# A hybrid encoder on one core: the sample's conv layer norm on the untransposed block, with its statistics sent through DRAM

## The chip, the core and the metric

The kernel runs on one core of one Trainium2 chip. A core has a matmul engine (PE, TensorE) and, beside it, DVE (VectorE), ACT (ScalarE) and POOL (GpSimd); SP (SyncE) issues nearly all DMAs of this kernel. Each engine takes its own instructions in order and waits on semaphores for the others. Matmul results land in PSUM, which is cut into eight banks of 128 x 512 numbers here; everything else is in SBUF, with 128 partitions. The metric is the time of one execution on the device, in microseconds.

## What is computed

One layer of an encoder, for two requests with the same weights: the prompt (512 tokens) and the sample (1024 tokens), in float32. The part that the change touches is the convolution branch.

```
def _layernorm(x, g, b):                     # over the 512 channels of one token
    mu = mean(x); xc = x - mu
    return xc * rsqrt(mean(xc * xc) + EPS) * g + b

h = rmsnorm(x); z = h @ w_in                 # q, k, v, ca, cb
a_out = window_attention(q, k, v)            # 512 channels
c = ca * sigmoid(cb)
c = dwconv(c, conv_dw_w, conv_dw_b)          # 31 taps along the tokens
c = silu(_layernorm(c, conv_ln_g, conv_ln_b))
x = x + concat([a_out, c]) @ w_out           # 1024 channels
h = rmsnorm(x); u = dwconv3(h @ w_up)        # 2 x 2816 channels
x = x + (silu(u_gate) * u_value) @ w_down
y = rmsnorm(x)
```

## The kernel before

Every float32 matmul is made of three: operands are split into a rounded high half and the rest (`hi`, `lo`), and hi x hi, hi x lo and lo x hi are summed in PSUM. ACT casts the high half, DVE or POOL subtracts for the low one.

The prompt's tokens are blocks 0 to 3 of 128 tokens, the sample's are blocks 4 to 11. First the input projection runs for all, then attention and the output projection of the prompt, then the prompt's up-projection (`up_half`, L983 and L987 its three-tap convolution) beside which the sample's attention (`scores`, `values`: L655 scores, L697 transposes, L711 and L712 values, L719 to L723 the result into `cat`) and the sample's long convolution run. Then come the sample's output projection (`out_half`, L813 to L815 on PE, one block and one half of the 1024 columns at a time, L819 adds the residual), and a long second half: up-projection and down-projection of the sample, both in a form with fewer products (L1249 to L1251 and L1612 to L1614 on PE).

The long convolution runs with channels on partitions; the sample's result goes to DRAM (`cvd`) in four chunks of 128 channels. The layer norm needs statistics over channels. `conv_norm(i)` therefore does the following for a block of 128 tokens:

- it loads the block from `cvd` into `held`, four chunks of (128 channels x 128 tokens), and the attention half from `catd`;
- L760: four transposes on PE turn it to tokens on partitions, into a PSUM bank `pt`;
- L765, L766: mean and variance per token on DVE; `rstd_of` (L147, L148) makes the reciprocal root on POOL;
- L769: DVE subtracts the mean and multiplies by the root, one number per partition each, into `xh`;
- after YN = 2 yields (other work is recorded between), L775: four transposes turn `xh` back to channels on partitions, into a second bank `p2`;
- L781: ACT applies gain and bias per channel, for the sample also putting the tokens in order (even and odd tokens were kept apart by the convolution); L782 to L785 make the swish and the two halves `cat[0]` (hi, by ACT's cast L784) and `cat[1]` (lo, L785 on DVE). The output projection reads these as its stationary operand for channels 512 to 1023 (kc 4 to 7).

The generator `fitted(i)` runs `conv_norm` for a sample block; blocks 4 and 5 are normalised in `tail()`, beside the end of the up-projection, blocks 6 to 11 in the loop over `turns_out`, NE = 2 blocks ahead of their output projection. The transposes use the bank `c` for blocks 4 and 5, then the banks `a`. Up to the second half a scheduler, which lists instructions by a model of their times, sets the order of each engine's instructions, PE's and SP's among them; only from the sample's up-projection on is PE's order fixed by hand. Tiles take slots of four sizes (`q`, `c`, `h`, `d`, and `s` for small ones), and a slot is free again when its holder is dropped.

Of the kernel before, what the change touches and what calls it, by code (L numbers as in the profile page):

```python
# [9 lines left out]
F32 = mybir.dt.float32  # L10
# [3 lines left out]
ALU = mybir.AluOpType  # L14

P = 128
# [8 lines left out]
CCH = 512  # L25
# [30 lines left out]
YN = 2  # L56
# [53 lines left out]
def tile_hybrid_encoder(ctx: ExitStack, tc: tile.TileContext, xs, rel_bias, norm_attn_g, w_in,  # L110
                        attn_sink, conv_dw_w, conv_dw_b, conv_ln_g, conv_ln_b, w_out, norm_ffn_g,
                        w_up, ffn_dw_w, ffn_dw_b, w_down, norm_final_g, onehot, laid, outs):
    nc = tc.nc
# [3 lines left out]
    dr = ctx.enter_context(tc.tile_pool(name="dr", bufs=1, space=bass.MemoryType.DRAM))  # L117
# [4 lines left out]
    sb = Slots(lambda tag: sml if tag[0] == "s" else big,  # L122
               dict(q=(15, 4096), c=(4, 4352), h=(61, 2048), d=(2, 2304), s=(33, 64)))
# [3 lines left out]
    def sm(n):  # L127
        return sb.tile([n])

    def bank(job):  # L130
        return banks.tile([NT], among=use[job])
# [8 lines left out]
    ident = cst.tile([P, P], F32, name="ident")  # L140
# [5 lines left out]
    def rstd_of(ss, n, out):  # L146
        nc.gpsimd.tensor_scalar(out, ss, 1.0 / n, EPS, op0=ALU.mult, op1=ALU.add)  # L147
        nc.gpsimd.tensor_tensor(out, out, nhalf[:, :out.shape[1]], op=ALU.pow)  # L148
# [95 lines left out]
    for _ in range(NW // 4):  # L244
        pt = bank("step")
        for i in range(4):
            nc.tensor.transpose(pt[:, i * P:(i + 1) * P], ident[:], ident[:])
        pt = None
# [60 lines left out]
    def drain(queue):  # L309
        while queue:  # L310
            advance(mid[0] if mid else queue)
# [368 lines left out]
    def cat_of(i, part):  # L680
        if (i, part) not in cats:
            cats[i, part] = (sb.tile([4, P], F32R), sb.tile([4, P], F32R))
        return cats[i, part]
# [55 lines left out]
    def load_cat(i):  # L739
        cats[i, 0] = (sb.tile([4, P], F32R), sb.tile([4, P], F32R))  # L740
        for L in range(2):
            nc.sync.dma_start(cats[i, 0][L][:].bitcast(F32), catd[blocks[i][1], :, L, :].rearrange("p (j t) -> p j t", t=P))

    def conv_norm(i):
        G, b = blocks[i]
        if G["g"] == 0:
            drain(convs)
        cat = cat_of(i, 1)
        if G["g"] == 0:
            cv = [kept[c][:, b * P:(b + 1) * P] for c in range(4)]  # L750
        else:
            held = sb.tile([4, P])
            nc.sync.dma_start(held[:].rearrange("p c (h k) -> p c h k", h=2), cvd[:, b])
            cv = [held[:, c, :] for c in range(4)]
            if (i, 0) not in cats:
                load_cat(i)
            yield 0.0
        pt = bank("norm")
        for c in range(4):
            nc.tensor.transpose(pt[:, c * P:(c + 1) * P], cv[c], ident[:])  # L760
        if G["g"] == 0 and b == G["nb"] - 1:
            kept.clear()
        held = None
        st, mv, rs = sm(6), sm(2), sm(1)
        nc.vector.bn_stats(st[:], pt[:])  # L765
        nc.vector.bn_aggr(mv[:], st[:])  # L766
        rstd_of(mv[:, 1:2], 1.0, rs[:])
        xh = sb.tile([CCH])
        nc.vector.tensor_scalar(xh[:], pt[:], mv[:, 0:1], rs[:], op0=ALU.subtract, op1=ALU.mult)  # L769
        del pt  # L770
        for _ in range(YN):
            yield 0.0
        p2 = bank("norm")
        for c in range(4):
            nc.tensor.transpose(p2[:, c * P:(c + 1) * P], xh[:, c * P:(c + 1) * P], ident[:])  # L775
        y, t = sb.tile([4, P]), sb.tile([4, P])
        for c in range(4):
            o, n = y[:, c, :], p2[:, c * P:(c + 1) * P]
            if G["g"] == 1:
                o, n = o.rearrange("p (k h) -> p h k", h=2), n.rearrange("p (h k) -> p h k", h=2)  # L780
            nc.scalar.activation(o, n, AF.Identity, scale=lng[:, c:c + 1], bias=lnb[:, c:c + 1])  # L781
        nc.scalar.activation(t[:], y[:], AF.Tanh)  # L782
        nc.vector.scalar_tensor_tensor(t[:], t[:], 1.0, y[:], op0=ALU.add, op1=ALU.mult)
        nc.scalar.copy(cat[0][:], t[:])  # L784
        nc.vector.tensor_tensor(cat[1][:], t[:], cat[0][:].bitcast(F32), op=ALU.subtract)  # L785
        yield 0.0
# [99 lines left out]
    def normed(i):  # L886
        yield from conv_norm(i)
        ready.add(i)
# [155 lines left out]
    def fitted(i):  # L1044
        yield from conv_norm(i)
        fit.add(i)
# [258 lines left out]
    st = {}  # L1305
# [610 lines left out]
```

## Time and profile before

| What | Value |
|---|---|
| median of 3 runs | 1481.91 us (1481.87 to 1482.33) |
| profiled execution, its own time | 1484.05 us |
| profiled execution, its span | 1482.1 us |
| mean granted clock of PE | 0.998 |
| DMA traffic | 228.17 MB, mean 154 GB/s |
| DMA, mean share of 16 engines, 630 to 650 us | 0.77 to 1.05 by stretches of 5 us |

Times in the profile are microseconds from the span's start. A timeline row has start, length, engine, line, operation, output and inputs by slot class, and in brackets how long the engine stood idle before it and what ended that. The chain row of a piece gives what it added to the chain of work that ended last. A row of the windows' table gives busy time and count of PE, of its weight loads, of DVE, ACT and POOL, then the granted clock as a share of full speed, the DMA share and GB/s.

### The profile page before, as it was taken

What the parts mean: (1) busy time and instruction counts of PE and PEld (TensorE: products, weight loads), DVE (VectorE), ACT (ScalarE), POOL (GpSimd) and SP (SyncE); (2) the same over time, 40 slices, a digit from 0 to 9 for tenths busy, and PEclk for the clock granted to TensorE, in tenths of its full rate; (3) what the DMA queues carried; (4) which work ended last, traced back from release to release, by engine and by line L of the source; (5) the groups of instructions that cost most, each with busy time, mean ns of one, the idle gap of its engine ahead of it and who ended that gap; (6) DMA issues with size and microseconds to landing.
All of it is one profiled execution on the core that took longest, in us unless ns stands there. A gap on an engine that the chain in (4) does not pass through costs nothing.

```text
span 1482.1 us, 19791 instructions
## 1 busy us (share of the span) xinstructions
PE 1464.6 (99%) x6688; PEld 1206.0 (81%) x6688; DVE 1117.9 (75%) x1502; ACT 805.8 (54%) x1434; POOL 803.8 (54%) x696
## 2 busy tenths in 40 slices
PE   9999999999999999999999999999999999999998
PEld 7788887878888888788887888888888888888886
DVE  6877945658998989666598888888886846578873
ACT  7534555458778677644565445444454553433355
POOL 3555453328888776422566666666655341135555
PEclk9999999999999999999999999999999999999999
DMA  9555331744444464373214433333333494356744
GB/s 368 191 152 145 110 101 36 244 161 142 122 142 135 136 192 136 110 282 123 84 58 142 150 129 127 131 124 123 123 126 96 147 337 152 125 190 220 228 166 156
DMA packets 124625, 228.17 MB, mean 154 GB/s; under 512 B 20420, under 2 KB 45764, under 8 KB 124397
## 3 DMA queue, kind: packets, MB, share of 16 engines
q1 hardware_dynamic: 124092, 226.37, 46.4%
q8 instruction: 52, 0.85, 0.2%
q10 hardware_dynamic: 432, 0.56, 0.1%
q14 instruction: 49, 0.39, 0.1%
HBM read 166.83 MB, written 61.10 MB: 154 GB/s over the span
## 4 chain that ended last, share of the span: by engine, by line
PE 88%; DVE 4%; DMA 2%; ACT 2%; issue 2%; POOL 1%; SPq 0%; POOLq 0%; ACTq 0%; DVEq 0%
PE w L1249 8%; PE w L1250 8%; PE w L1251 8%; PE w L1613 7%; PE w L1614 7%; PE w L1612 7%; PE b L317 4%; PE u L317 4%; PE b L318 4%; PE u L318 4%; PE u L319 4%; PE b L319 4%; PE a L655 1%; PE a L697 1%; PE u L813 1%
## 5 line engine op out<-in xcount | busy, mean ns | idle before, releaser
L164 POOL TENSOR_TENSOR q<-q,q 128x1024 fp32r<-128x1024 f32 x64 | 154.4, 2413 | 69.4 <-ACT q L163 48.7
L1102 POOL TENSOR_TENSOR q<-q,q 128x512 fp32r<-128x512 f32 x82 | 125.4, 1538 | 115.2 <-ACT q L1235 115.2
L1102 DVE TENSOR_TENSOR h<-h,h 128x512 fp32r<-128x512 f32 (+1 forms) x161 | 132.6, 854 | 55.9 <-ACT h L1110 23.7
L1612 PE MATMUL w<-h,h 128*128 128x512 f32 x432 | 168.0, 389 | 0.0
L1614 PE MATMUL w<-h,h 128*128 128x512 f32 x432 | 168.0, 389 | 0.0
L1613 PE MATMUL w<-h,h 128*128 128x512 f32 x412 | 160.3, 389 | 0.0
L1102 POOL TENSOR_TENSOR h<-h,h 128x512 fp32r<-128x512 f32 (+1 forms) x46 | 67.9, 1478 | 141.7 <-ACT h L1595 119.6
L1249 PE MATMUL w<-h,q 128*128 128x512 f32 x350 | 137.7, 393 | 1.1 <-ACT w L1320 0.9
L1251 PE MATMUL w<-h,q 128*128 128x512 f32 x350 | 136.4, 390 | 0.1
L1250 PE MATMUL w<-h,q 128*128 128x512 f32 x350 | 136.3, 389 | 0.0
L1110 ACT CAST h<-h 128x512 fp32r<-128x512 f32 x116 | 69.2, 620 | 106.0 <-DVE h L1102 30.5
L317 PE MATMUL b<-h,q 128*128 128x512 f32 x312 | 123.2, 395 | 1.5 <-ACT h L466 0.9
L318 PE MATMUL b<-h,q 128*128 128x512 f32 x312 | 122.8, 393 | 0.0
L319 PE MATMUL b<-h,q 128*128 128x512 f32 x312 | 122.6, 394 | 0.0
L317 PE MATMUL u<-h,q 128*128 128x512 f32 x272 | 107.3, 395 | 0.8 <-DVE h L983 0.8
L319 PE MATMUL u<-h,q 128*128 128x512 f32 x272 | 107.2, 394 | 0.0
L318 PE MATMUL u<-h,q 128*128 128x512 f32 x272 | 107.2, 394 | 0.0
L357 DVE SCALAR_TENSOR_TENSOR c<-d,cvw,c 128x512 f32<-128x512 f32 x128 | 95.8, 749 | 1.5
L163 ACT CAST q<-q 128x1024 fp32r<-128x1024 f32 x66 | 69.0, 1046 | 49.0 <-PE b L318 13.3
L1612 PEld LDWEIGHTS w<-h,h 128*128 128x128 f32 x432 | 81.1, 188 | 16.9
L1614 PEld LDWEIGHTS w<-h,h 128*128 128x128 f32 x432 | 81.1, 188 | 16.6
L348 POOL TENSOR_TENSOR h<-h,h 128x512 f32<-128x512 f32 x62 | 82.1, 1326 | 20.9 <-ACT h L347 16.6
(501 smaller groups left out, 4011.1 us busy)
## 6 DMA issues: line engine op xcount, KB each, us to landing
q<-in_laid_w_up SPq DMA_DIRECT2D x88, 512.0 KB, 3.8
ga<-q SPq DMA_DIRECT2D x65, 256.0 KB, 2.2
h<-gap SPq DMA_DIRECT2D x57, 256.0 KB, 3.8
h<-ga SPq DMA_DIRECT2D x57, 256.0 KB, 3.5
h<-in_w_down SPq DMA_DIRECT2D x52, 256.0 KB, 3.5
q<-in_laid_w_in SPq DMA_DIRECT2D x22, 512.0 KB, 4.0
gap<-h SPq DMA_DIRECT2D x42, 256.0 KB, 2.6
q<-in_x_sample SPq DMA_DIRECT2D x15, 512.0 KB, 7.7
```

What stands on the lines that cost most here:

```text
L164: (nc.vector if dve else nc.gpsimd).tensor_tensor(lo[:], raw[:], hi[:].bitcast(F32), op=ALU.subtract)
L317: nc.tensor.matmul(out, whi[:, kc, :], hi[:], start=(kc == 0), stop=False)
L318: nc.tensor.matmul(out, whi[:, kc, :], lo[:], start=False, stop=False)
L319: nc.tensor.matmul(out, wlo[:, kc, :], hi[:], start=False, stop=(kc == KC - 1))
L357: nc.vector.scalar_tensor_tensor(acc[:], src(t), w(t), acc[:], op0=ALU.mult, op1=ALU.add)
L1102: (eng or nc.vector).tensor_tensor(out, a, b, op=ALU.subtract)
L1249: nc.tensor.matmul(out, whi[:, s], hi[:], start=(start and c == 0), stop=False, **go)
L1250: nc.tensor.matmul(out, whi[:, s], lo[:], start=False, stop=False, **go)
L1251: nc.tensor.matmul(out, wlo[:, s], hi[:], start=False, stop=(stop and c == 3), **go)
L1612: nc.tensor.matmul(out, sh[:, c], th[:], start=(p == 0 and not seeded), stop=False, **go)
L1613: nc.tensor.matmul(out, sh[:, c], tl[:], start=False, stop=False, **go)
L1614: nc.tensor.matmul(out, sl[:, c], th[:], start=False, stop=(p == NPAIR - 1), **go)
```

## The change

For the sample's blocks the normalisation is done on `held`, the block as loaded. The four transposes for the statistics stay. Mean and reciprocal root of the 128 tokens, a tile of 128 partitions x 2, are stored to a small DRAM tensor `lnd` as two rows of 128, and loaded again with every partition receiving both rows (`wide`). DVE then subtracts the row of means from all four chunks, POOL multiplies by the row of roots, and ACT reads the result where it used to read the bank `p2`. The transposes back are gone for these blocks, and `pt` is given up before the trip. `held` is dropped only after ACT has read it. The prompt's blocks are normalised as before.

```diff
+    lnd = [dr.tile([2, P], F32, name=f"lnd{b}") for b in range(8)]
+
+    def spread_stats(b, mv):
+        rstd_of(mv[:, 1:2], 1.0, mv[:, 1:2])
+        nc.sync.dma_start(lnd[b][:].rearrange("s p -> p s"), mv[:])
+        wide = sb.tile([2, P])
+        nc.sync.dma_start(wide[:], lnd[b][:].partition_broadcast(P))
+        return wide
...
-        held = None
-        st, mv, rs = sm(6), sm(2), sm(1)
+        st, mv = sm(6), sm(2)
         nc.vector.bn_stats(st[:], pt[:])
         nc.vector.bn_aggr(mv[:], st[:])
-        rstd_of(mv[:, 1:2], 1.0, rs[:])
-        xh = sb.tile([CCH])
-        nc.vector.tensor_scalar(xh[:], pt[:], mv[:, 0:1], rs[:], op0=ALU.subtract, op1=ALU.mult)
-        del pt
-        for _ in range(YN):
-            yield 0.0
-        p2 = bank("norm")
-        for c in range(4):
-            nc.tensor.transpose(p2[:, c * P:(c + 1) * P], xh[:, c * P:(c + 1) * P], ident[:])
+        if G["g"] == 1:
+            del pt
+            wide = spread_stats(b, mv)
+            for _ in range(YN):
+                yield 0.0
+            nc.vector.tensor_tensor(held[:], held[:], wide[:, 0:1, :].to_broadcast([P, 4, P]), op=ALU.subtract)
+            nc.gpsimd.tensor_tensor(held[:], held[:], wide[:, 1:2, :].to_broadcast([P, 4, P]), op=ALU.mult)
+            del wide
+            p2 = held[:].rearrange("p c t -> p (c t)")
+        else:
...
             nc.scalar.activation(o, n, AF.Identity, scale=lng[:, c:c + 1], bias=lnb[:, c:c + 1])
+        held = None
```

Lines of the changed kernel have other numbers. There L748 is the store to `lnd`, L750 the load, L769 the transposes for the statistics, L773 and L774 the statistics, L780 the subtraction, L781 the multiplication, L799 the scaling, L801 the tanh, L802 to L804 the rest of the swish and the two halves (L803 ACT's cast); L832 to L834 are the output projection, L838 its residual, L868 and L869 the cast and subtraction that split w_out.

The scheduler also lists the work around it in another order, from block 4 to block 11 (some 600 to 730 us); before and behind that the order stays. In the extracts a name is slot, serial number and a second number: the banks of PSUM are a, b, c, u, all other letters are SBUF or DRAM.

PE around the first use of block 5's normalised half. In the kernel before, `h13_1065` is that half (hi) and `u1_349` and `b0_352` are the two column halves of block 5's output, `u0_350` the second half of block 4's:

```order
L813 MATMUL u0_350_6674<-h11_1112_6662,d1_1039_6266 128x512
L815 MATMUL b0_352_6730<-h48_1104_6633,h46_1064_6419 128x512
L813 MATMUL b0_352_6730<-h40_1106_6650,h15_1063_6418 128x512
L814 MATMUL b0_352_6730<-h39_1107_6651,h15_1063_6418 128x512
L813 MATMUL u1_349_6600<-h58_1012_6125,h13_1065_6422 128x512
L814 MATMUL u1_349_6600<-h10_1013_6126,h13_1065_6422 128x512
```

In the changed kernel `h46_1064` is block 5's normalised half (hi), `c0_347` the first column half of its output, `a1_349` and `a2_352` the statistics banks of blocks 6 and 7, `b1_353` and `b0_351` the output of block 6:

```order
L834 MATMUL b0_351_6788<-h21_1005_6101,h27_1120_6694 128x512
L769 MATMUL a1_349_6703<-ident_82,h33_1118_6691 128x128 x4
L769 MATMUL a2_352_6801<-ident_82,h6_1133_6778 128x128 x4
L832 MATMUL b1_353_6840<-h23_1100_6625,h17_1119_6693 128x512
L833 MATMUL b1_353_6840<-h20_1101_6626,h17_1119_6693 128x512
L834 MATMUL b1_353_6840<-h23_1100_6625,h27_1120_6694 128x512
L832 MATMUL c0_347_6602<-h58_1012_6133,h46_1064_6427 128x512
L833 MATMUL c0_347_6602<-h10_1013_6134,h46_1064_6427 128x512
```

Between the statistics transposes of block 5 and this first use stand 63 matmuls of 512 columns and 16 transposes in the kernel before, 49 and 16 in the changed one; and the transposes of blocks 6 and 7 now stand together, ahead of it.

DVE behind block 5's statistics, in the kernel before (`s4_1072` and `s10_1073` are block 5's statistics, `h48_1075` its normalised block):

```order
L765 BN_STATS s4_1072_6448<-c0_339_6443 128x6
L766 BN_AGGR s10_1073_6449<-s4_1072_6448 128x2
L983 SCALAR_TENSOR_TENSOR q12_1083_6527<-u0_342_6477,fw_264,q12_1083_6527 128x511
L769 TENSOR_SCALAR h48_1075_6455<-c0_339_6443,s10_1073_6449,s11_1074_6450 128x512
L983 SCALAR_TENSOR_TENSOR q12_1083_6527<-u0_342_6477,fw_264,q12_1083_6527 128x511
L721 TENSOR_TENSOR q6_1082_6516<-a0_341_6466,h42_1068_6426 64x512
L700 TENSOR_TENSOR h38_1088_6554<-a1_346_6548,h34_1087_6553 128x512
```

In the changed kernel, from block 5's subtraction on (`q3_1073` and `h32_1140` are the loaded rows of blocks 5 and 7, `h60_1103` the low half of a piece of w_out):

```order
L780 TENSOR_TENSOR h48_1066_6429<-h48_1066_6429,q3_1073_6460 128x512
L773 BN_STATS s10_1121_6708<-a1_349_6703 128x6
L773 BN_STATS s14_1138_6806<-a2_352_6801 128x6
L774 BN_AGGR s11_1122_6709<-s10_1121_6708 128x2
L774 BN_AGGR s15_1139_6807<-s14_1138_6806 128x2
L802 SCALAR_TENSOR_TENSOR q0_1078_6506<-q0_1078_6506,q2_1077_6505 128x512
L721 TENSOR_TENSOR q6_1080_6518<-a0_340_6471,h42_1067_6431 64x512
L804 TENSOR_TENSOR h13_1065_6428<-q0_1078_6506,h46_1064_6427 128x512
L869 TENSOR_TENSOR h34_1107_6657<-h24_1095_6615,h18_1106_6656 128x512
L869 TENSOR_TENSOR h16_1109_6661<-h25_1096_6617,h38_1108_6660 128x512
L780 TENSOR_TENSOR h6_1133_6778<-h6_1133_6778,h32_1140_6813 128x512
L721 TENSOR_TENSOR h14_1090_6593<-a0_346_6574,h42_1067_6431 64x512
```

Right behind the last row stands the split L869 that makes `h60_1103`. The statistics of blocks 6 and 7 have moved behind block 5's subtraction, and this split behind block 7's.

SP's queue at the same place, in the kernel before:

```order
L1116 DMA q11_1085_6537<-in_norm_ffn_g 128x1024
L152 DMA q3_1086_6539<-in_x_sample 128x1024
L753 DMA h33_1120_6689<-cvd_159 128x512
L152 DMA q0_1174_6999<-in_x_sample 128x1024
L1007 DMA gap24_3314<-q14_1084_6531 128x512
```

and in the changed one:

```order
L152 DMA q13_1091_6600<-in_x_sample 128x1024
L748 DMA lnd1_1273<-s4_1072_6454 128x2x1
L762 DMA h33_1118_6691<-cvd_159 128x512
L1026 DMA gap24_3322<-q11_1082_6533 128x512
L152 DMA q14_1154_6896<-in_x_sample 128x1024
L750 DMA q3_1073_6460<-lnd1_1273 128x256
L152 DMA q11_1137_6786<-in_x_sample 128x1024
L1135 DMA q3_1083_6539<-in_norm_ffn_g 128x1024
L748 DMA lnd2_1274<-s11_1122_6709 128x2x1
```

Block 5's store and load now stand in SP's order, with three other DMAs between them, and the load of norm_ffn_g behind both.

More of the change, by code (lines that the diff above doesn't have):

```diff
@@ L762, in conv_norm @@
             kept.clear()
-        held = None
-        st, mv, rs = sm(6), sm(2), sm(1)
+        st, mv = sm(6), sm(2)
         nc.vector.bn_stats(st[:], pt[:])
         nc.vector.bn_aggr(mv[:], st[:])
-        rstd_of(mv[:, 1:2], 1.0, rs[:])
-        xh = sb.tile([CCH])
-        nc.vector.tensor_scalar(xh[:], pt[:], mv[:, 0:1], rs[:], op0=ALU.subtract, op1=ALU.mult)
-        del pt
-        for _ in range(YN):
-            yield 0.0
-        p2 = bank("norm")
-        for c in range(4):
-            nc.tensor.transpose(p2[:, c * P:(c + 1) * P], xh[:, c * P:(c + 1) * P], ident[:])
+        if G["g"] == 1:
[8 more added lines that the diff above has]
+        else:
+            rs, xh = sm(1), sb.tile([CCH])
+            rstd_of(mv[:, 1:2], 1.0, rs[:])
+            nc.vector.tensor_scalar(xh[:], pt[:], mv[:, 0:1], rs[:], op0=ALU.subtract, op1=ALU.mult)
+            del pt
+            for _ in range(YN):
+                yield 0.0
+            p2 = bank("norm")
+            for c in range(4):
+                nc.tensor.transpose(p2[:, c * P:(c + 1) * P], xh[:, c * P:(c + 1) * P], ident[:])
         y, t = sb.tile([4, P]), sb.tile([4, P])
```

## Prediction

> **What bounds the kernel now.** I read the page first (busy shares and the chain that ended last), then PE's waits and its timeline where the changed work lies, then that stretch on the other engines, and last the landing times of the DMAs.
>
> ```profile
> span 1482.1 us, 19791 instructions
> PE 1464.6 (99%) x6688; PEld 1206.0 (81%) x6688; DVE 1117.9 (75%) x1502; ACT 805.8 (54%) x1434; POOL 803.8 (54%) x696
> PE 88%; DVE 4%; DMA 2%; ACT 2%; issue 2%; POOL 1%; SPq 0%; POOLq 0%; ACTq 0%; DVEq 0%
> ```
>
> PE is busy for 99% of the span and carries 88% of the chain, so an instruction taken off PE is worth its own time wherever PE runs without a gap, and an operand that arrives late costs its lateness. DVE, ACT and POOL have room on average; what counts is when each result is ready.
>
> The sample's eight layer norms (blocks 4 to 11) run between 610 and 712 us. PE there, in the timeline (start, length, and in brackets the idle time before):
>
> ```profile
> 620.16 0.39 PE L712 MATMUL a<-h,h 128*128 128x512 f32 x1
> 622.54 0.50 PE L655 MATMUL a<-q,h 128*128 128x256 f32 x2 [0.61 <-DVE h L721]
> 623.80 0.66 PE L697 MATMUL a<-ident,h 128*128 128x128 f32 x4 [0.76 <-DVE s L659]
> 625.21 0.53 PE L317 MATMUL u<-h,q 128*128 128x512 f32 x1 [0.76 <-DVE h L983]
> 628.93 0.39 PE L317 MATMUL u<-h,q 128*128 128x512 f32 x1
> 633.03 0.39 PE L813 MATMUL b<-h,h 128*128 128x512 f32 x1
> 646.26 0.39 PE L813 MATMUL c<-h,h 128*128 128x512 f32 x1
> 648.75 0.39 PE L815 MATMUL c<-h,h 128*128 128x512 f32 x1
> ```
>
> From 646.26 to 648.75 are 11 steps in a row, 0.226 us each: PE's pace. Only at 622 to 625 does it wait, 2.13 us in three pieces. Behind that wait it runs slowly: 9 steps from 625.21 to 628.93 take 3.72 us instead of 2.04. The table by stretches shows why (its column behind the busy times is the granted clock):
>
> ```profile
> 625.00:630.00 5.00, 4.79 (x14) 3.86 (x15) 4.89 (x12) 4.47 (x12) 0.19 (x1) 0.66 0.37 116
> ```
>
> So a wait of some 2 us has cost 1.7 us more in half-clock time.
>
> **What is taken off PE.** Each sample block loses the four transposes that turned the normalised tile back (L775). The chain of waits counts such a group by what it adds:
>
> ```profile
> 643.66 0.44 PE c L775 x4
> ```
>
> 8 blocks by 0.44 us are 3.5 us. Block 4's group (620.62) stands just ahead of the wait at 622.54. What ends that wait starts at L712, ahead of the removed group, and goes on through ACT and DVE:
>
> ```profile
> 620.59 0.58 ACT L719 COPY h<-a 64x512 f32<-64x512 f32 x1 [5.66 <-PE a L712]
> 622.60 0.75 DVE L983 SCALAR_TENSOR_TENSOR h<-u,fw,h 128x511 f32<-128x511 f32 x1
> ```
>
> PE would only wait 0.44 us longer there, so 7 groups count: -3.1 us. On DVE the normalisation of a PSUM tile (0.81) becomes a subtraction in SBUF (0.68, below): nothing. ACT scales as before, from SBUF. POOL gets 8 multiplications of about 1.29 us, 10 us in all on an engine with 54% load.
>
> **What is added: a way through DRAM.** Per block: a store of 128x2 numbers, a load that waits for it, the subtraction, the multiplication. Block 5 in the present kernel, from its statistics to the first part of the result, in the timelines:
>
> ```profile
> 636.92 0.60 PE L760 MATMUL c<-ident,h 128*128 128x128 f32 x4
> 637.84 0.69 DVE L850 TENSOR_TENSOR h<-h,h 128x512 fp32r<-128x512 f32 x1 [1.03 <-ACT h L849]
> 638.45 0.69 DVE L765 BATCH_NORM_STATS2 s<-c 128x6 f32<-128x512 f32 x1
> 639.17 0.18 DVE L766 BATCH_NORM_AGGREGATE s<-s 128x2 f32<-128x6 f32 x1
> 639.44 0.19 POOL L147 TENSOR_SCALAR s<-s 128x1 f32<-128x1 f32 x1 [4.71 <-DVE s L766]
> 639.72 0.57 POOL L148 TENSOR_TENSOR s<-s,nhalf 128x1 f32<-128x1 f32 x1
> 640.32 0.81 DVE L769 TENSOR_SCALAR h<-c,s,s 128x512 f32<-128x512 f32 x1 [0.31 <-DMA q<-in_x_sample]
> 644.14 1.52 ACT L781 ACTIVATE q<-c,vecs 128x128 f32<-128x128 f32 x4 [2.97 <-PE c L775]
> 646.70 0.58 ACT L719 COPY h<-a 64x512 f32<-64x512 f32 x1
> 647.30 0.63 ACT L782 ACTIVATE q<-q 128x512 f32<-128x512 f32 x1
> 649.09 0.62 ACT L784 CAST h<-q 128x512 fp32r<-128x512 f32 x1
> 643.50 0.68 DVE L1005 TENSOR_TENSOR q<-b,q 128x512 f32<-128x512 f32 x1
> 669.91 1.29 POOL L1102 TENSOR_TENSOR c<-q,c 128x512 fp32r<-128x512 f32 x1 [2.93 <-ACT c L1235]
> ```
>
> When PE needs it: in the changed order (first pair of extracts above) the output projection of block 5 reads the cast result after 12 matmuls of block 4, four transposes, and then 49 matmuls and 16 transposes. From 633.03, which the wait at 622.54 fixes in both kernels, that is 61 x 0.226 + 0.44 + 4 x 0.44 = 16.0, so 649.0. In the present order the same use stands 14 matmuls further behind the statistics, which is where the cast at 649.09 fits.
>
> When it is ready: the second L850 still stands ahead of the statistics on DVE, so the square root ends at about 640.3 as now. The two DMAs are nowhere in this trace; the nearest rows of the DMA view (size, median us to landing; the last three are of the windows 636 to 640 and 640 to 645):
>
> ```profile
> ga<-q SPq DMA_DIRECT2D x65, 256.0 KB, 2.2
> cvd<-h SPq DMA_DIRECT2D x8, 256.0 KB, 3.0
> q<-cvd SPq DMA_DIRECT2D x1, 256.0 KB, 2.7
> h<-cvd SPq DMA_DIRECT2D x1, 256.0 KB, 7.9
> q<-in_norm_ffn_g SPq DMA_DIRECT2D x1, 512.0 KB, 7.0
> q<-in_x_sample SPq DMA_DIRECT2D x1, 512.0 KB, 5.0
> ```
>
> The store: between 2.2 (a quiet store) and 7.9 (what was issued at 639.23, behind 512 KB loads). I take 3.0, the store in the smallest pieces, because two of the large loads that were ahead of it at 639 (norm_ffn_g and one of x) now stand behind it in SP's order. The load: between 2.7 and 7.9; I take 5.0, what was issued at about its time, since in SP's order a cvd load, a gap store and a 512 KB load of x go between the two. So: 640.3 + 3.0 + 5.0 = 648.3; subtraction 0.68, multiplication 1.29: 650.3; then on ACT the four scalings 1.52, the tanh 0.63, two attention copies of 0.58 that still stand between, the cast 0.62, 3.9 in all: 654.2. PE would wait 5.2 us. With the short ends (2.2, 2.7) it is 2.1, with the long one for the load too (7.9) 8.1, with both long 13.0.
>
> A wait of 5.2 is longer than the 2.13 that cost half-clock time at 625, so I add 1.7 again. On this the Trainium skill (TensorE: Matmul & The Clock Gate, Part 1: The HAM clock gate) says that the array falls to half clock after an idle window of about 3.4 us and comes back after a busy one; the 0.66 over 5 us agrees with one such window, though 2.13 us of idling in pieces was enough here. By that page up to two windows could be slow, and the sum below would be an estimated 1.7 us higher.
>
> **What queues behind.** DVE takes its work in order. Behind block 5's subtraction stand the statistics of blocks 6 and 7; behind block 7's subtraction stands the low half of a piece of w_out (L869 h60) that PE needs 19 matmuls after it leaves the first wait. Block 7: load of block 5 landed 648.3, subtraction 0.68, two statistics 1.74, two square roots on POOL 1.52, store 3.0, load 2.7, subtraction 0.68, an attention difference and the split of 0.68 each: 660.0. PE gets there at 654.2 + 4.3 = 658.5, or 660.2 with the half clock. A bound of 0 below and, if norm_ffn_g's 512 KB that now go ahead of this store hold it up (7.0 for 3.0), 4 above; I take 1.0. On SP, loads of x, cvd and catd behind the stores leave some us later; the next such use lies over 10 us off, so they cost nothing while the store itself isn't late. Block 4's trip (square root at 613.5, few DMAs) ends near 619, before the DVE work at 621.79 that PE waits for: nothing.
>
> **The sum.** -3.1 + 5.2 + 1.7 + 1.0 = +4.8 us. The profiled execution took 1484.05 us with its span of 1482.1; the median of the runs shown is 1481.91, close to the span, so I put the difference on the median: 1486.7.
>
> **The rivals.** First, faster: the trip is hidden everywhere and only the transposes' time is left, 1481.9 - 3.1 = 1478.8. For it speaks PE's 99%, and that every block is normalised about two blocks ahead. It needs block 5's load at 643.1, a trip of 2.8 us, or its statistics about as much earlier; the quiet rows alone make 4.9.
>
> Second, no change: both DMAs take their quiet times, PE waits 2.1 us and keeps its clock: 1480.9. A page speaks for it: the Trainium skill (DMA: Bandwidth & Descriptors, Anatomy of one DMA) gives each transfer a fixed 2.0 us plus bytes at 436 GB/s, and says that it is mostly the write's receipt; that would be 4.3 us for both, a wait of 1.5 and an estimated 1480.3. Against it stands the 7.9 at this very place, which no fixed cost explains.
>
> Third, much slower: DVE's order makes the trips follow one another, for block 8's subtraction stands ahead of block 9's statistics and so on. One round is statistics 0.87, square root 0.76, store, load and subtraction 0.68; a block's output projection on PE is 48 x 0.226 = 10.9 us. From store plus load of 8.6 us on PE runs out of blocks. With 7.9 + 5.0 each block loses 4.3 us; over five blocks 21, less the block's worth that is ahead (10.9): 10 us on top, 1497. The DMAs are light after 655, which speaks against it.
>
> **Chances.** My forecast 0.53 (its own range 1483.5 to 1492), faster 0.14, no change 0.18, much slower 0.15. The runs shown lie 0.5 us apart; I call 0.2%, 3 us, what a measurement can tell. Faster is the first rival, 0.14; within 0.2% the second, 0.18; slower the rest, 0.68. For 8 in 10 the range leaves out the third rival and a little around the first: 1478.7 to 1494.0.
>
> **What would show it.** A wait of PE of 2 to 8 us near 649, at the first matmul of block 5 that reads its normalised half (L832, on the ACT cast L803), with the granted clock near 0.6 behind it; the subtraction L780 waiting for a DMA on DVE, with the statistics of blocks 6 and 7 starting right after it; lnd's load of block 5 landing at about 648; a second, short wait near 660 on L869. PE's instructions are fewer by 32. I am wrong if the landing is below 644 (then the first or second rival), if PE comes to block 5 several us later than 649, or if new waits stand at blocks 8 to 11.

## The result, and the profile after

The changed kernel takes 1542.15 us (median of 5 runs, 1540.13 to 1546.52) against 1482.33 (1481.87 to 1483.51) for the kernel before on the same chip: ratio 1.0406, 95% interval 1.0389 to 1.0423. It is 60 us slower, where I forecast 5. The profiled execution took 1542.28 us with its span of 1540.5.

The page after: span, busy shares, and the chain of work that ended last.

```profile
span 1540.5 us, 19765 instructions
PE 1478.4 (96%) x6656; PEld 1213.5 (79%) x6656; DVE 1113.1 (72%) x1502; ACT 807.1 (52%) x1434; POOL 812.4 (53%) x704
PE 79%; DMA 8%; DVE 6%; ACT 2%; POOL 2%; issue 2%; SPq 0%; POOLq 0%; DVEq 0%; ACTq 0%
```

DMA has risen from 2% to 8% of the chain. PE has 32 matmuls less, yet is busy 13.8 us longer: it runs at half clock for a while (granted clock 0.50 from 630 to 635 us). Its waits between 605 and 800 us (who waits for whom: us in total, times, longest):

```profile
PE u L1151 <- ACT h L1164: 10.6, 1, 10.6
PE a L655 <- DVE h L721: 7.4, 1, 7.4
PE a L769 <- DMA h<-cvd: 6.9, 2, 3.6
PE c L832 <- ACT h L803: 6.5, 1, 6.5
PE b L832 <- ACT h L803: 5.6, 2, 3.8
PE u L833 <- DVE h L869: 5.1, 1, 5.1
PE u L832 <- ACT h L803: 4.2, 1, 4.2
```

With the short ones that is 47 us, against 2.4 before beside the same work. The span grew by 58.4: 45.0 more waiting, less 3.5 for the removed transposes, so about 17 are left for half-clock time. PE's busy time says the same: 13.8 us more with 3.5 us less to do. The table by stretches shows both (PE's busy time first; the granted clock stands ahead of the last two columns):

```profile
620.00:640.00 20.00, 11.68 (x43) 8.82 (x42) 10.82 (x22) 8.98 (x20) 2.90 (x4) 0.74 0.52 151
660.00:680.00 20.00, 8.42 (x23) 5.78 (x21) 8.14 (x14) 6.88 (x13) 6.17 (x8) 0.59 0.33 105
760.00:780.00 20.00, 9.51 (x35) 7.88 (x36) 11.10 (x13) 9.71 (x19) 9.29 (x8) 0.66 0.16 47
```

What PE waits for comes from the new way through DRAM. The DMA view from 605 to 775 us (size, median us from issue to landing), and DVE's waits there:

```profile
lnd<-s SPq DMA_DIRECT2D x8, 1.0 KB, 8.0
h<-lnd SPq DMA_DIRECT2D x7, 128.0 KB, 4.7
...
DVE h L780 <- DMA h<-lnd: 43.9, 5, 11.0
DVE h L780 <- DMA q<-lnd: 11.5, 1, 11.5
DVE q L780 <- DMA h<-lnd: 9.8, 1, 9.8
```

The store of 1 KB takes 8.0 us in the median, and DVE stands still for 65 us in seven waits before the subtraction. The chain shows one round and the start of the next (start, what it added):

```profile
702.23 9.86 DMA lnd<-s
712.11 3.47 DMA h<-lnd
715.60 0.70 DVE h L780
716.42 1.28 POOL h L781
718.06 0.56 POOL s L148
718.64 8.45 DMA lnd<-s
727.11 4.70 DMA h<-lnd
731.82 0.69 DVE h L780
```

Subtraction, the next block's root, its store, its load, its subtraction: in this chain nothing overlaps. The last four subtractions start at 715.60, 731.82, 748.45 and 766.05, 16 to 18 us apart, where PE needs 10.9 us for a block.

The store is slow with nothing beside it. Block 4's store and load on SP (start, length), and DVE at that place:

```profile
612.87 0.37 SPq L748 DMA_DIRECT2D lnd<-s  x1
620.56 0.32 SPq L750 DMA_DIRECT2D h<-lnd  x1
...
615.67 0.68 DVE L1024 TENSOR_TENSOR d<-b,h 128x512 f32<-128x512 f32 x1
626.12 0.69 DVE L780 TENSOR_TENSOR q<-q,h 128x512 f32<-128x512 f32 x1 [9.76 <-DMA h<-lnd]
```

And the DMA engines in the same time (their mean busy share is the last column but one):

```profile
613.00:614.00 1.00, 0.77 (x4) 0.29 (x3) 1.00 (x3) 0.95 (x2) 0.10 (x1) 1.00 0.15 1
614.00:615.00 1.00, 1.00 (x6) 0.87 (x7) 1.00 (x2) 0.26 (x1) 0.00 (x0) 1.00 0.00 0
617.00:618.00 1.00, 1.00 (x6) 0.84 (x5) 0.00 (x0) 0.00 (x0) 0.00 (x0) 1.00 0.00 0
```

All pieces have left within a microsecond (share 0.15 between 613 and 614); then almost nothing moves, and the load can only be issued at 620.56. So the 7.6 us that the DMA view gives this store from issue to landing are neither a queue nor bandwidth. What is left is the time until the writes are confirmed, for which the profile has no row of its own. On this the Trainium skill (DMA: Bandwidth & Descriptors, Anatomy of one DMA) says, of DMAs issued from GpSimd, that most of a transfer's fixed 2.0 us is the receipt of the target memory's write. The trace, of a DMA issued from SP, agrees in that nearly all of the time lies behind the pieces' movement, but it is over 6 us here.

### The profile page after: what moved, and what is told of

The parts are those of the page before. It is cut to its first block, busy times and chain, and to the rows that moved or that the text cites. A ratio compares the mean times of both kernels' runs of the same rounds, so it can differ in the third digit from the quotient of the medians.

```text
span 1540.5 us, 19765 instructions
## 1 busy us (share of the span) xinstructions
PE 1478.4 (96%) x6656; PEld 1213.5 (79%) x6656; DVE 1113.1 (72%) x1502; ACT 807.1 (52%) x1434; POOL 812.4 (53%) x704
## 4 chain that ended last, share of the span: by engine, by line
PE 79%; DMA 8%; DVE 6%; ACT 2%; POOL 2%; issue 2%; SPq 0%; POOLq 0%; DVEq 0%; ACTq 0%
PE w L1268 7%; PE w L1269 7%; PE w L1270 7%; PE w L1632 6%; PE w L1633 6%; PE w L1631 6%; PE b L317 4%; PE u L317 4%; PE b L318 4%; PE b L319 4%; PE u L318 4%; PE u L319 4%; DMA lnd<-s 4%; PE a L655 1%; PE a L697 1%
## 5 line engine op out<-in xcount | busy, mean ns | idle before, releaser
L1121 DVE TENSOR_TENSOR h<-h,h 128x512 fp32r<-128x512 f32 (+1 forms) x161 | 127.9, 825 | 53.3 <-ACT h L1129 21.8
```

The source lines that it names most:

```text
L1121: (eng or nc.vector).tensor_tensor(out, a, b, op=ALU.subtract)
```

## The experiments

My theory from this profile: the store is slow by its form, and as DVE takes its work in order, the trips stand end to end. The rivals: the rest of the change costs by itself; the store is slow because of what runs beside it; SP's order, not DVE's, makes the queue.

**The trip taken out (early_rows).** The statistics aren't stored; the load reads two rows of x, so the block's own mean and root are left out. As the subtraction then depends on neither, the scheduler also lists PE, DVE, ACT and POOL in another order than in the change.

```
-        nc.sync.dma_start(lnd[b][:].rearrange("s p -> p s"), mv[:])
-        nc.sync.dma_start(wide[:], lnd[b][:].partition_broadcast(P))
+        nc.sync.dma_start(wide[:], GR[1]["x"][0:2, 0:P].partition_broadcast(P))
```

> The change without the trip: nothing is stored, and the two rows are loaded from the first two rows of x, so the load waits for nothing (the block's own mean and root are left out of the result). Theory (the trip's length in DVE's order is the whole loss): the waits of PE at blocks 4 to 11 fall from 46 us to under 3, and the time is 1478.8 to 1483, that is 1481.9 less up to 3.1 for the transposes. Rival (the new places of work on SP, DVE and POOL, and the multiplication that now stands between the subtraction and ACT, cost time by themselves): waits of 10 us and more remain, 1492 or above.

1480.36 us, ratio 0.9989 (0.998 to 0.9998), 2.2 us less than the 1482.56 before. PE's longest wait between 600 and 800 us:

```profile
PE a L655 <- DVE h L721: 1.1, 1, 1.1
```

The theory holds: without the trip, the subtraction, the multiplication on POOL and the order that the scheduler then makes cost nothing, and the transposes' time comes back, as far as it can be measured. So the 60 us come with the trip. Whether the change's own order would cost nothing without it isn't shown, since no kernel has that order without the wait.

**The store alone (store_only).** The kernel before, with the stores added on SP and read by nobody; the order of PE, DVE, ACT and POOL stays.

```
         rstd_of(mv[:, 1:2], 1.0, rs[:])
+        if G["g"] == 1:
+            nc.sync.dma_start(lnd[b][:].rearrange("s p -> p s"), mv[:])
```

> The kernel before, with the eight stores of 128x2 numbers (256 pieces of 4 B) added and read by nobody. Theory (the store itself is slow, by its pieces): each lands 6 to 9 us after its issue also where no other transfer is under way, and the time stays within 0.2% (1480 to 1485), as nothing waits for them. Rival (the store was slow because of the transfers beside it, or because of what waited): it lands in 2 to 4 us where the DMAs are quiet, and long only next to 512 KB loads.

The landing was longer than expected, 11.4 us, and the time was a miss: 1495.38 us, ratio 1.0088 (1.0073 to 1.0103), 12.8 us lost although nothing reads what is stored. The DMA view from 600 to 800 us, first of this kernel, then the same transfers of the kernel before:

```profile
lnd<-s SPq DMA_DIRECT2D x8, 1.0 KB, 11.4
h<-cvd SPq DMA_DIRECT2D x7, 256.0 KB, 7.5
x1d<-q SPq DMA_DIRECT2D x7, 512.0 KB, 7.0
```

```profile
h<-cvd SPq DMA_DIRECT2D x7, 256.0 KB, 3.2
x1d<-q SPq DMA_DIRECT2D x7, 512.0 KB, 2.7
```

Other transfers land 4 us later. PE's longest wait, 5.2 us at 683.49, leads back through DVE, POOL and ACT to a load of w_up that landed 9.4 us after its issue. So there is a second mechanism that my theory lacked: a store that is confirmed late holds up what runs with it.

**From another queue (store_act).** The same stores issued by ACT (`nc.scalar.dma_start`).

> The kernel before with the eight stores added in their first form (two rows of 512 B, 256 pieces of 4 B, read by nobody), issued by ACT in place of SP. On SP they cost 12.8 us, since the loads and stores issued behind them landed late (cvd 7.5 us in place of 3.2). Theory (a store whose writes are confirmed late holds up the completion of what runs behind it on the same DMA engines, whichever engine issued it): 1490 to 1498, cvd's loads again at 5 us or more. Rival (only transfers of the same queue are held up): 1481 to 1486, cvd near 3.2 us.

1501.98 us, ratio 1.0125 (1.0106 to 1.0145), above the expected 1490 to 1498, with cvd's loads at 7.0 us. The hold-up doesn't go by the issuing engine. That the time is 7 us above store_only's says nothing of the queue, since the scheduler lists PE, DVE and ACT in another order here. On this the Trainium skill (DMA: Bandwidth & Descriptors, Queues, rings and completion order) says that a transfer's semaphore increment lands only after every earlier write of the same DMA engine, whichever queue it came from; both runs agree with that, 7.0 and 7.5 us for loads that took 3.2.

**Other forms of the store (store_own, store_apart).** Again 256 pieces of 4 B, unread, but each starts 8 B behind the one before it, where it was 4 B: first with a partition's two numbers beside each other (neighbouring partitions are then 16 B apart), then in two rows (neighbouring partitions 8 B apart).

```
store_own:   lnd [P, 2, 2];  store to lnd[b][:, :, 0]
store_apart: lnd [2, P, 2];  store to lnd[b][:, :, 0].rearrange("s p -> p s")
```

> The kernel before with the eight stores added, read by nobody, as 256 pieces of 4 B again, but a partition's two numbers lie 8 B apart in DRAM, so each DMA engine writes a stretch of 128 B of its own; in the form of the change two rows of 512 B are shared out in pieces of 32 B per engine. Theory (number of pieces of 4 B): landing and time as with the first form of these stores, 9 to 12 us and 1492 to 1498. Rival (engines that write next to each other in the same short stretch of DRAM hold each other up): landing of 3 to 5 us and 1481 to 1487.

> The kernel before with the eight stores added on SP, read by nobody, as two rows again, but with the numbers of a row 8 B apart, so that the rows are 1 KB long and an engine writes 64 B of each in place of 32 B. Theory (neighbouring engines that write into the same stretch of 64 B hold each other up): landing of 3 to 6 us and 1481 to 1487, as with a partition's numbers side by side. Rival (it is the two rows per partition, or the number of pieces): 9 to 12 us and 1491 to 1498.

store_own: 1484.39 us, ratio 1.0011 (1.0002 to 1.002), landing 5.3 us. store_apart: 1483.52, ratio 1.0009 (1.0 to 1.0019), landing 5.1. The number of pieces, which was the theory of the first run and the rival of the second, falls, and the spacing decides: with pieces 8 B apart in place of 4, the store's cost goes from 12.8 us to under 3, in the same order on every engine. cvd's loads still land late, 5.6 and 5.4 us against 3.2, so a delay of 2 us costs little here and one of 4 us much. Why the spacing decides stays open: the expectations speak of DMA engines that write close to each other, but no trace here shows which engine writes which bytes.

**The change with quicker stores (pairs, two_rows).**

```
pairs:    lnd [P, 2];  store to lnd[b][:] (128 pieces of 8 B); rows read as wide[:].rearrange("p t s -> p s t")
two_rows: nc.tensor.transpose(pt[0:2, 0:P], mv[:], ident[:]); nc.scalar.copy(two[0:2, :], pt[0:2, 0:P]); store two[0:2, :]
```

> The change with mean and root side by side in DRAM: the store has 128 pieces of 8 B in place of 256 of 4 B; the load is as large as before, its rows are read with a stride. Theory (time by the number of pieces): halfway between 8.0 and a quiet store's 2.4, so a landing of about 5.2 us; some 2.8 us less in each of seven rounds, 20 us in all, so 1515 to 1530. Rival (time by the pieces' smallness, whatever their number, or a fixed delay): the landing stays at 7 to 8 us and the time at 1535 to 1545.

> The change with the statistics turned into two rows first (one transpose on PE, one copy on ACT), so that the store has 2 pieces of 512 B in place of 256 of 4 B. Theory (pieces): the store lands in 2 to 3.5 us, one round is about 0.9 + 0.8 + 1 + 2.5 + 4.7 + 0.7 = 10.6 us, just under the 10.9 us of a block's products, so PE waits under 10 us and the time is 1480 to 1492. Rival (a store that is waited for is slow whatever its form): it lands in 7 to 8 us and the time is 1530 to 1550.

pairs: 1513.05 us, ratio 1.0203 (1.0188 to 1.0219); two_rows: 1497.55, ratio 1.0101 (1.0087 to 1.0114). The first lies 2 us under its range, the second 5 over. The DMA view of pairs from 600 to 800 us, and block 4's store and load on SP there, and in two_rows:

```profile
lnd<-s SPq DMA_DIRECT2D x8, 1.0 KB, 3.8
...
612.37 0.32 SPq L748 DMA_DIRECT2D lnd<-s  x1
615.24 0.32 SPq L750 DMA_DIRECT2D h<-lnd  x1
```

```profile
613.88 0.25 SPq L751 DMA_DIRECT2D lnd<-h  x1
615.03 0.34 SPq L753 DMA_DIRECT2D h<-lnd  x1
```

At the same quiet place the load follows the store after 7.7 us in the change, 2.9 with pairs and 1.2 with two long pieces. DVE's waits for the rows fall with it, from 65 us to 36 and 15, and the loss from 60 us to 30 and 15. What the quickest still loses I put down to the load's 4 us and the rest of the round, which stand in order as before, and to a wait of PE of 2.4 us for the root at the added transpose.

**More lead (n3y3, pairs_n3y3, n3y3_act).** Each norm starts three blocks ahead (NE = 3, block 6 joins `tail()`), with YN = 3.

> The change with each norm started three blocks ahead in place of two and a step more between the statistics and the subtraction; the store stays at 256 pieces. On DVE the statistics now mostly stand two and two, with two subtractions behind them, so one round of waiting serves two blocks. Theory (trips follow one another in DVE's order): PE waits about half as much as with the change, and the time is 1505 to 1520. Rival (each store costs PE its time by holding up other transfers, wherever the subtraction stands): 1530 or above.

> Mean and root side by side in DRAM (the form that took 1513.1) and three blocks ahead with one step more before the subtraction (which made the change slower, 1557.7). Theory (it was the store's 8 us, with SP waiting behind it, that turned the lead into a loss): with a store of 3 to 4 us the lead pays, and the time is 1490 to 1507. Rival (the lead costs by itself, since it brings the first trips into the busier end of the attention): 1513 or above.

> Three blocks ahead, as in the run before that took 1557.7, with the stores issued by ACT in place of SP. There the second store of a pair stood on SP behind the load that waited for the first (statistics ready at 669.97, store issued at 677.15). Theory (SP's order, beside DVE's, makes the trips follow one another): stores leave at once, a pair of blocks shares one round, and the time falls by 10 to 25 us, to 1533 to 1548. Rival (SP's order is not what counts; DVE's order and the slow store are enough): 1552 to 1562.

n3y3: 1557.68 us, ratio 1.0508 (1.0494 to 1.0523), slower than the change and in the range of the rival; the expectation was wrong. pairs_n3y3: 1515.03, ratio 1.0221 (1.0204 to 1.0238), no better than pairs, again in the rival's range. n3y3_act: 1550.94, ratio 1.0464 (1.0441 to 1.0487). One reason why the lead doesn't pay shows on SP in n3y3, beside the statistics of the second block on DVE and its root on POOL:

```profile
666.87 0.38 SPq L748 DMA_DIRECT2D lnd<-s  x1
676.73 0.32 SPq L750 DMA_DIRECT2D h<-lnd  x1
677.15 0.37 SPq L748 DMA_DIRECT2D lnd<-s  x1
...
669.79 0.18 DVE L774 BATCH_NORM_AGGREGATE s<-s 128x2 f32<-128x6 f32 x1
670.33 0.55 POOL L148 TENSOR_TENSOR s<-s,nhalf 128x1 f32<-128x1 f32 x1
```

What the second store sends is complete with the root, at 670.88, but the store leaves at 677.15, behind the load that waits for the first store: SP is a second engine that puts trips end to end. (The expectation of n3y3_act counts from the statistics, 669.97.) Issuing the stores from ACT took back 6.7 us, which lies between the two expectations; how the wait divides between DVE's and SP's order stays open.

**The subtraction on POOL (pool_waits).** The root after the load, on 128x128, and the subtraction on POOL.

> The change with the root taken after the load (on POOL, 128x128) and the subtraction on POOL too, so that no instruction of DVE waits for a load of the statistics, and a block's store follows its statistics at once. Store and load are as in the change. Theory (DVE's order makes the trips follow one another; beside that the stores hold up other transfers, which by themselves cost 12.8 us): 1492 to 1508, with DVE's waits for loads gone. Rival (SP's order, where each load of statistics waits for its store with everything behind it, sets the pace): 1520 or above, with PE's waits as long as with the change.

1633.12 us, ratio 1.1014 (1.0997 to 1.1031), far above the theory's range, and it tells nothing about the orders:

```profile
L781 POOL TENSOR_TENSOR h<-h,nhalf x7: 20715/20751/21422, 628.3 to 838.7; 128x128 f32<-128x128 f32 x7
```

The power takes POOL 20.75 us in the median (the row has minimum, median and maximum in ns) for 128 numbers per partition, where the profile of before had 0.57 for one.

**Statistics three blocks earlier (ahead_pairs3, ahead_rows3).** A generator `stats_ahead(b)` loads the block, takes its statistics and stores them; `conv_norm` later loads the block again, with the rows.

> The statistics of a block are taken three blocks of norm work earlier, from a load of the block of their own (eight loads of 256 KB more), and stored side by side (128 pieces of 8 B); the norm itself later loads the block and the two rows together, and subtracts and multiplies as in the change. Between a block's store and its load stand other blocks, so nothing waits for the store. Theory (what still made the form with pairs 30 us slower than before is the trip's length, which the orders of DVE and SP put end to end): PE's waits go below 4 us and the time is 1478.5 to 1485. Rival (the transfers themselves, or the larger number of them, hold up the rest): 1490 to 1513.

> The same with the store in the form of the change (two rows, 256 pieces of 4 B, engines side by side in stretches of 64 B). Theory (two costs: the trip's length, gone here, and the hold-up of the transfers behind the store, which alone cost 12.8 us): 1488 to 1500. Rival (without a wait for the store its slowness is hidden): 1478.5 to 1485.

1503.66 us, ratio 1.0136 (1.0121 to 1.0151), and 1534.5, ratio 1.0351 (1.0334 to 1.0368). The first lies in the range of its rival, that the transfers themselves or their larger number hold up the rest; the second lies above both of its ranges. DVE waits for the rows only 4.9 us now (in ahead_pairs3), but the second load of each block brings waits of its own. PE's largest there are

```profile
PE u L844 <- ACT h L815: 5.5, 1, 5.5
PE c L752 <- DMA h<-cvd: 3.1, 1, 3.1
```

So the two runs leave open what the trip's length costs.

**The dependence cut (cut_pairs, cut_rows).** Every transfer stays, as many and as large; only the load reads x in place of `lnd`. So the block's own statistics are left out, and the subtraction waits for neither statistics, root nor store. Here too the scheduler makes another order than in the change: PE, DVE, ACT and POOL work in the order of early_rows.

```
cut_rows:  nc.sync.dma_start(wide[:], GR[1]["x"][0:2, 0:P].partition_broadcast(P))
cut_pairs: the same from GR[1]["x"][0, 0:2 * P], viewed as (p s)
```

> The form with pairs, where the store stays as it is (128 pieces of 8 B) but the 128 x 256 numbers that the norm reads are loaded from x, as 1 KB in one row, so that the load waits for no store (the block's own statistics are left out of the result). The transfers are as many and as large as in the form that took 1513.1. Theory (the remaining 30 us are the wait for a trip, end to end): 1479 to 1486. Rival (the store and the load hold up other transfers, wherever they are waited for): 1495 to 1513.

> The change, where the store stays as it is (256 pieces of 4 B in two rows) but the two rows that the norm reads are loaded from x and wait for no store (the block's own statistics are left out of the result). Theory (of the 60 us about a fifth is the hold-up of other transfers behind the store, the rest the wait for the trip): 1480.4 + 12.8, so 1489 to 1498. Rival (only the wait for the trip counts in the changed kernel): 1479 to 1486; another (the hold-up is most of it): 1510 or above.

The times, beside those from above:

| kernel | store | load waits for it | us | ratio (95%) |
|---|---|---|---|---|
| early_rows | none | no | 1480.36 | 0.9989 (0.998 to 0.9998) |
| cut_pairs | 8 B pieces | no | 1485.3 | 1.0013 (1.0004 to 1.0023) |
| pairs | 8 B pieces | yes | 1513.05 | 1.0203 (1.0188 to 1.0219) |
| cut_rows | 4 B pieces in two rows | no | 1508.45 | 1.0171 (1.0154 to 1.0188) |
| the change | 4 B pieces in two rows | yes | 1542.15 | 1.0406 (1.0389 to 1.0423) |

Between early_rows and cut_rows only the eight stores on SP differ, so slow stores cost 28 us (1508.45 - 1480.36) through the transfers that they hold up, more than the fifth of the loss that I expected. The wait for the trip, with the order that the scheduler makes for it, brings another 34 (1542.15 - 1508.45). With the quick store it is 5 and 28. How the loss of the change itself divides isn't shown: there SP stands still for 55 us before the loads of the rows, so less is under way behind a store, and cvd's loads land in 3.5 us. In cut_rows, DMA view, PE's largest wait, and block 4's load of the rows on SP with the subtraction on DVE that waits for it:

```profile
lnd<-s SPq DMA_DIRECT2D x8, 1.0 KB, 8.8
h<-cvd SPq DMA_DIRECT2D x7, 256.0 KB, 9.2
h<-in_x_sample SPq DMA_DIRECT2D x7, 128.0 KB, 8.3
...
PE u L833 <- DVE h L869: 10.8, 1, 10.8
...
613.33 0.37 SPq L750 DMA_DIRECT2D h<-in_x_sample  x1
623.11 0.69 DVE L780 TENSOR_TENSOR q<-q,h 128x512 f32<-128x512 f32 x1 [7.33 <-DMA h<-in_x_sample]
```

Block loads and the rows' loads now land as late as the store beside them, though they need nothing from it. Block 4's load of the rows left one microsecond behind the store (612.30) and landed 9.7 us later; in cut_pairs, behind the quick store, the same load took 3.1.

**Without DRAM (pe_spread).** Mean and root, repeated along a row, are turned on PE and copied by ACT to `wide`.

```
+        for s in range(2):
+            nc.tensor.transpose(pt[:, s * P:(s + 1) * P], mv[:, s:s + 1].to_broadcast([P, P]), ident[:])
+        nc.scalar.copy(wide[:].rearrange("p s t -> p (s t)"), pt[:, 0:2 * P])
```

> The change with no way through DRAM: mean and root of a block, repeated along the row, are turned on PE (two transposes of 128x128 per block) and copied by ACT to the tile that the subtraction and the multiplication read. PE has 2 transposes per block less than before, 8 x 0.22 = 1.8 us. Theory (the trip was the whole loss): PE's waits stay under 3 us at blocks 4 to 11, and the time is 1479.5 to 1483. Rival (the chain statistics, root, turn, copy, subtraction, multiplication, scalings is too long for two blocks ahead even without DRAM, and PE stands still at the turn, as it did for 2.4 us in the form with two rows): 1485 to 1495.

1482.13 us, ratio 0.9998 (0.9989 to 1.0007), with no wait of PE over 1.1 us: as fast as before. Two transposes per block less (1.8 us) are below what can be told from nothing. No form tried that computes the norm beats the kernel before by a measurable amount.

## Why the prediction was wrong

The step that failed is the store's price, 3.0 us where 8.0 was measured, and with it two terms that the sum put at nothing: the trips that follow one another (rounds of 16 to 18 us where PE needs 10.9 for a block), and the transfers that a late store holds up (28 us where nothing waits for it). In detail:

- **The transposes, -3.1.** In keeping: without the trip the kernel is 0.3 to 3.0 us faster (the interval of early_rows).
- **The store's price, 3.0 between 2.2 and 7.9. This step failed.** I took it from stores of 256 KB, and blamed the 7.9 on what was queued ahead. It measures 8.0 in the median, 7.6 where the DMAs are idle, and up to 11.0. No row of before showed a store whose rows are cut into pieces of 4 B, so the bounds had no claim on it; a kernel that is the one before with the store added would have.
- **The load, 5.0.** Right: 4.7.
- **Block 4's trip at nothing ("ends near 619"). Failed with the store.** Its subtraction starts at 626.12 (row above), L721 behind it, and PE waits 7.4 us there; block 5's store leaves at 646.45, not 640.3.
- **The first wait of block 5, 5.2 near 649.** The right instruction (L832 on the cast L803), 6.5 us, but it ends at 667.43. PE came there at 660.9, twelve us later than forecast, for block 4's wait, one of 3.4 us for a load of cvd at 657.72, and half clock between them; that was one of the signs of being wrong that the prediction named.
- **The second wait, on L869, 1.0 near 660.** The right instruction again, 5.1 us, ending at 679.98.

```profile
667.43 0.79 PE L832 MATMUL c<-h,h 128*128 128x512 f32 x1 [6.50 <-ACT h L803]
679.98 0.80 PE L833 MATMUL u<-h,h 128*128 128x512 f32 x1 [5.08 <-DVE h L869]
```

- **The clock, 1.7.** About 17 us, as the waits are many.
- **The loads behind the stores on SP, which "cost nothing while the store itself isn't late".** Failed with its condition: the store is late. Where nothing waits for it, loads are held up not on SP but after issue, and cut_rows puts 28 us on that. Nothing in the profile of before points to this; the rule of the Trainium skill quoted at store_act does.
- **The third rival, 0.15.** Its mechanism is what the chain shows: trips one after another, from a store and load of 8.6 us on, here 12.7. What I held against it, that the DMAs are light after 655, was no argument, since the store needs no neighbours to be slow. Its 1497 was worked out with a trip of 12.9 us, almost the measured one, and counted only the five blocks behind the first ones, 4.3 us each; the rounds were 16 to 18 us, 5 to 7 over a block's 10.9, since the subtraction, the next root and SP's issue come on top, and PE had already waited 7.4 us at block 4 and 6.5 at block 5.

## What to carry to other kernels

Price a trip through DRAM by its smallest pieces and by how closely they lie in DRAM, not by its bytes: the same 1 KB took from 1.2 us (two pieces, to the load that waits for it) to a median of 11.4 (256 pieces, beside other work). Where an engine that works in order waits for a trip, ask whether the next trip's first half stands behind that wait, on the engine that computes and on the one that issues the DMAs: then the trips add up. The attempts here to move the first halves ahead brought costs of their own, so what that could win isn't shown. And add the new transfer to the old kernel, unread, before building on it: what it costs then is what it does to the others.

## What the runs showed of the hardware

- A 1 KB store as 256 pieces of 4 B in two rows lands in 7.6 us on idle DMAs, of which the pieces' movement is under 1 us; with its pieces 8 B apart in place of 4 the median was 5.1 to 5.3 in place of 11.4 beside the same work, and as 128 pieces of 8 B it was 3.8 in the changed kernel.
- Eight such stores, read by nobody, made the kernel 12.8 us slower, with cvd's loads landing in 7.5 us in place of 3.2; from ACT's queue it was 19.9, with another order on PE, DVE and ACT.
- POOL's power on 128x128 numbers takes 20.75 us, on 128x1 0.57.
